# A hybrid decoder step: a later Mamba transpose, cross-attention behind the pages, longer pauses at two joins, residual loads in two parts

## The chip, the cores and the metric

The kernel runs on 1 core of a Trainium2 chip. The metric is the device time of one execution in microseconds; the time of a kernel is the median of its runs. The core has five engines with a queue of instructions each, run in order: PE (TensorE, matrix multiplication), DVE (VectorE), ACT (ScalarE), POOL (GpSimd) and SP (SyncE, which here only issues DMAs). POOL and ACT issue some DMAs too.

## The reference

One layer of a decoder step for 1024 prompt tokens and 8 sample tokens. The hidden rows are normalized and projected by `w_in`; the columns go to four head groups, each output is gated, and `w_out` and a residual follow.

```python
h = rmsnorm(x, lp['norm_g'])
p = h @ lp['w_in']
dq, dk, dvv, dg, rs, rg, mz, mxbc, mdt, xq, xg = split_in(p)
# A: differential attention (samples: over 512 paged past positions)
out_a = rmsnorm(o, subln_g) * (1 - lam_init) * silu(dg)
# B: RWKV-7, a scan over time of an 8-head state
y, rw_state_new = rwkv7_scan(rh, exp(logw), kh, vh, -kk, kk * ah, rw_state)
# M: Mamba-2, causal conv on x/B/C, then a chunked scan
ym, ssm_new = ssd_scan(xh * dt, A * dt, bh, chh, ssm_state, chunk)
# X: cross-attention into 256 memory tokens
s = einsum('bqhd,bmhd->bhqm', qx, mem_k) * D_X ** -0.5
out_x = einsum('bhqm,bmhd->bqhd', softmax(s), mem_v) * silu(xg)
x = x + concatenate([out_a, out_b, out_m, out_x]) @ lp['w_out']
# then the final rmsnorm of all rows
```

D_MODEL is 2048, each group is 512 wide, and the projection has 6792 columns.

## The kernel before

**Projections as filler.** The 1032 token columns stand in three groups of 344. Each float32 operand is split in a high and a low part (`hh`, `hl` for the activations, `whi`, `wlo` for a piece of weights), so each product takes three matmuls of 344 columns (line 565). A block is 128 output columns for all groups; a piece is a quarter of it (`KP` = 4 of 16 row tiles), loaded to `raw`, split by ACT (`whi`, line 541) and DVE (`wlo`, line 542) one piece ahead. Blocks run in the order of `ORDER`: attention's, `xq`, `rs` (RWKV), `mdt`, `mxbc`, `mz`, and last the twelve gates `xg`, `dg`, `rg`. Each block is evacuated by an `Ev...` class to DRAM. The 53 blocks of the projections (and a narrow one, `mdt`) are followed by those of `w_out`.

**Lanes and the planner.** The mixers are Python generators, called lanes. `Driver.run` lays out the program: it keeps a planned time `K.now`, which each matmul raises by its estimate (344 / 2400 us for a projection matmul), and a lane that yields a number rests for so many planned us. While no lane is due, a batch of projection matmuls is laid out (8, 4 or 10, by stage). `yield None` asks again later; `K.mark` and `K.wait` tie lanes together. So a pause becomes a number of projection matmuls between two steps of a lane in PE's queue. A scheduler then orders each engine's queue by priority and by what it takes to be ready: work whose inputs it takes to be there, DMAs above all, may stand ahead of its place in the program. Loads and splits of weights have the higher priority (`K.hi`).

**Stages.** In turn: memory and hidden rows; attention (`mixer_a`); `lane_x` (prompt's cross-attention, `mixer_x`) with `lane_sa` (`samples_a`, then `samples_x`); RWKV (`Rwkv.lanes` with `lane_b`); `lane_dt`; `lane_m` (`mixer_m`, prompt's Mamba) with `lane_s` (`samples_m`); `output`. Each stage ends when its lanes end; projections left over run on into the next, and the last of them are drained in `output`.

**What the change touches.**
- `samples_m` (from line 1375): loads `xs` (`smx`, line 1380), copies it to `v` (`smv`, lines 1381 and 1382, DVE), rests, and transposes it on PE (`p_sm`); its rows go to DRAM (`svM`) and from there the sample's state steps are fed. `mixer_m` beside it scans `r8` on DVE (line 1282), multiplies by the masked `gm` (1290, 1293), forms `xdt` (1303), and after a rest runs `p_yd` on PE from both.
- `Rwkv.products`: for each of 16 units, after the gram products, `at`, `x0`, `lt` (line 953) and `gs` are formed, then a rest, then the first join (16 matmuls to `p_t`). Four more joins follow in a loop, each after `lt` (line 973, DVE) and `rt` (line 979, ACT) and a rest.
- `samples_a`: gathers 32 pages of keys by POOL (`sakp`), multiplies and reduces each on DVE (lines 1634, 1635), six pages behind; 38 rests of 1.5 or 2.1. Then `p_sas` and the softmax. `samples_x` does the same with 16 pieces of memory keys (`sxkp`, lines 1765, 1766) and rows `sxqb` that pass through DRAM. `mixer_x` runs 16 steps: `p_xs`, softmax (`xm`, `xe`), `p_xt`, `xpt`, `p_xo`.
- PSUM: `K.ps(name, 0)` takes a buffer of a ring of three, `K.ps(name, 1)` of a ring of two.
- `output`: `residual` loads the residual rows of the first two groups (`xo`, line 1864), `evm` are the gated, mixed activations loaded and split anew (line 1873), `EvOut.rows` transposes an output block (`p_out`) and adds it to `xo`. The tiles of `xo` lie in a pool that takes the memory of the Mamba stage's pools; those of `evm` take the slots of the third group's activations, which the last block of the projections frees.

Of the kernel before, what the change touches and what calls it, by code (L numbers as in the profile page):

```python
# [11 lines left out]
F32 = mybir.dt.float32  # L12
# [819 lines left out]
class Rwkv:  # L832
# [69 lines left out]
    def products(self):  # L902
# [10 lines left out]
        for it in range(self.UNITS):  # L913
# [48 lines left out]
            for h in range(2):  # L962
                nc.vector.tensor_tensor(gs[:, h], pg[h], gm, op=ALU.mult)
            yield 4.0
            pt = ps("p_t")
# [3 lines left out]
            for l in range(4):  # L969
                xc = P.tile([128, nb, 32], F32, name="xc", tag="tm")  # L970
                nc.vector.transpose(flat(xc), pt[:, nb * 32:nb * 64])  # L971
                lt = P.tile([128, nb, 64], F32, name="lt", tag="lt")
                nc.vector.tensor_tensor(lt.rearrange("p j (k t) -> p j k t", k=2),  # L973
                                        xc.unsqueeze(2).to_broadcast([128, nb, 2, 32]),
                                        mt[:, l].rearrange("p (k t) -> p k t", k=2).unsqueeze(1).to_broadcast([128, nb, 2, 32]),
                                        op=ALU.mult)
                rt = P.tile([128, 2, nb, 32], F32, name="rt", tag="rt")
                m = 2 if l < 3 else 1
                nc.scalar.copy(rt[:, :m].rearrange("p a j t -> p (a j t)"), pt[:, :m * nb * 32])  # L979
                yield 1.6 if l else 2.2  # L980
                for b, h, q, w, n in bh:
                    K.mm(ptv[q, :m, b, :], lhsT=lt[q, b, :], rhs=rt[q, :m, b, :], start=False, stop=b == nb - 1,
                         skip_group_check=True)
# [391 lines left out]
def samples_m(K, P, dt):  # L1375
# [6 lines left out]
    nc.vector.tensor_copy(out=v[:, 32:64].rearrange("p (b s) -> p b s", b=4), in_=xs[:, 4:8, :])  # L1382
    yield 1.50
    p = K.ps("p_sm", 1)
# [201 lines left out]
def samples_a(K, P):  # L1586
# [36 lines left out]
    for i in range(32 + 6):  # L1623
# [13 lines left out]
        yield 2.1 if i >= 6 else 1.5  # L1637
    yield 2
    p = K.ps("p_sas", 0)
    for g in range(4):  # L1640
# [98 lines left out]
def samples_x(K, P):  # L1739
# [5 lines left out]
    yield 4.50  # L1745
    p = K.ps("p_sxx", 1)
    K.tp(p[:32, :128], x.rearrange("p s h -> p (s h)"), K.id)
# [20 lines left out]
    yield 8.92  # L1768
    p = K.ps("p_sxs", 1)
    for a in range(2):  # L1770
# [8 lines left out]
    yield 2.5  # L1779
    p = K.ps("p_sxw", 1)  # L1780
    for a in range(2):
# [5 lines left out]
    for b in range(8 + 3):  # L1787
# [9 lines left out]
        if b % 4 == 0:  # L1797
            po = K.ps("p_sxo", 1)
        for a in range(2):
# [4 lines left out]
        if b % 4 == 3:  # L1804
            yield from value_columns(K, P, po, o, b // 4, 1, tag="vce")
    nc.sync.dma_start(out=K.so[12:16, :, T:TT].rearrange("b p t -> p b t"), in_=o.rearrange("p (b s) -> p b s", b=4))
# [3 lines left out]
class EvOut:  # L1810


    def __init__(self, cb, xo, ss, done, fg=None, late=0.0):
        self.cb, self.xo, self.ss, self.done, self.fg, self.late = cb, xo, ss, done, fg, late

    def __call__(self, K, g, p):
# [4 lines left out]
    def rows(self, K, g, e):  # L1821
        nc, cb = K.nc, self.cb
        yield 2.0 + self.late
        q = K.ps("p_out", g % 2)
        for k in range(3):
# [20 lines left out]
def output(K, D):  # L1846
    nc, I = K.nc, K.I
    PC = 256
    with K.tc.tile_pool(name="op", bufs=1) as P:
# [6 lines left out]

        def residual():
            for g in range(2):
                for k in range(3):
                    src, n = rows[g, k]  # L1860
                    xo[g, k] = P.tile([128, 2048], F32, name=f"xo_{g}_{k}", tag="xo", bufs=6)
                    for c in range(0, 2048, 1024):
                        for p0, r, ap in src:
                            nc.sync.dma_start(out=xo[g, k][p0:p0 + r, c:c + 1024], in_=ap[:, c:c + 1024])
                        yield 4.00

        D.run([residual()], all_acc=True)
        with K.hi():
# [6 lines left out]
        def last_group():  # L1875
            yield 0.72
            for kt in kts:
                e = K.ev.tile([128, G + 3], F32, name="evm", tag="ev")[:, :G]
                nc.sync.dma_start(out=e, in_=K.sm[kt][:, 2 * G:])
                K.split_act(kt, 2, e, None)  # L1880
                yield 4.0

        def tokens(g, k, cb):
# [34 lines left out]
        def blocks():  # L1918
            K.ahead, K.more = AHEAD, P
            for cb in range(16):  # L1920
                fc = P.tile([128, 128], F32, name="fgc", tag="fgc", bufs=2)
                nc.sync.dma_start(out=fc, in_=I["final_g"][:, cb * 128:cb * 128 + 128].to_broadcast([128, 128]))
                yield from K.block(I["w_out"], cb * 128, [0, 1], EvOut(cb, tokens, ss, done, lambda cb, t=fc: t), KO_OUT)

# [15 lines left out]
            for cb in range(16):  # L1940
                if cb == FINCB:
                    while not fin:
                        yield False
                    K.large, K.ahead = (lambda: P.tile([128, 16, 128], F32, name="oraw", tag="xo", bufs=6)), 8
                yield from K.block(I["w_out"], cb * 128, [2], EvOut(cb, tokens, ss, done, gain, 4.0 if cb < 2 else 0.0),
                                   KO_OUT)
                K.turn += 1

        D.acc = blocks()
        D.run([last_group()], all_acc=True)  # L1950
        for k in range(3):
# [57 lines left out]
def lane_x(K):  # L2009

    pool = lambda n: K.tc.tile_pool(name=n, bufs=1)
    yield from K.wait("xq3", 9.00)
    with pool("xap") as P:
        a, b = mixer_x(K, P, (0, 1)), mixer_x(K, P, (2, 3))
# [124 lines left out]
```

## Time and profile before

| | |
|---|---|
| median of 3 runs | 2157.95 us (2156.27 to 2159.46) |
| the profiled execution | 2159.76 us |
| its span, first to last instruction | 2158.0 us |
| PE busy | 2088.2 us (97%) |
| DVE busy | 1145.3 us (53%) |
| ACT busy | 840.9 us (39%) |
| POOL busy | 201.7 us (9%) |
| mean granted clock of PE | 0.990 |

How to read it: "busy" is the time in which an engine had at least one instruction under way. A matmul's pipelined end is modelled, so a busy PE isn't PE at its peak. An idle time is put down to what ended last by the profile ("<-"); "issue" there means that the profile shows no releaser. The granted clock is 1.00 at PE's higher level (2.4 GHz) and 0.50 at its lower one (1.2 GHz). Of 70 us in which PE was idle, some 17 lie in the first 100 us and at the end, which the change doesn't touch.

### The profile page before, as it was taken

The numbers are of one execution on the slowest core, as the hardware profiler recorded it, in microseconds if no ns is written. First come the engines' busy times: TensorE is split into PE (matmuls) and PEld (weight loads), VectorE is DVE, ScalarE is ACT, GpSimd is POOL, SyncE is SP. The second block draws the span as 40 slices with busy tenths as digits, with TensorE's granted clock in tenths as the row PEclk, the third lists the DMA queues.
The fourth block names the chain that finished last, engine by engine and source line by source line (L and its number), as shares of the span: only waits on it lengthen the run. The fifth ranks groups of instructions, "written<-read, shape, count | busy, mean of one in ns | idle before, by whom it ended". The sixth has DMA issues, their size and how long they took to land. (4 is left out here: it accounts for less than half of the span.)

```text
span 2158.0 us, 41612 instructions
## 1 busy us (share of the span) xinstructions
PE 2088.2 (97%) x16260; PEld 1981.2 (92%) x16260; DVE 1145.3 (53%) x2795; ACT 840.9 (39%) x2231; POOL 201.7 (9%) x286
## 2 busy tenths in 40 slices
PE   8999999999999999999999999998999999999997
PEld 6799999999989999988888888897999999999997
DVE  6814353543743252258977776655865354333554
ACT  6724353443223312145455444431121144333544
POOL 2100000000721220011110001001100000000000
PEclk9999999999999999999999999998999999999998
DMA  7643435242843572333222222226544583222781
GB/s 257 194 135 87 129 88 140 78 118 68 257 144 106 154 220 68 89 85 80 74 58 67 55 62 56 58 77 159 157 136 139 153 263 106 74 69 73 241 249 53
DMA packets 336925, 263.12 MB, mean 122 GB/s; under 512 B 62204, under 2 KB 310986, under 8 KB 336032
## 3 DMA queue, kind: packets, MB, share of 16 engines
q1 hardware_dynamic: 323744, 218.64, 35.8%
q0 software_dynamic: 12320, 40.28, 6.1%
q8 instruction: 128, 2.10, 0.4%
q10 hardware_dynamic: 664, 1.54, 0.2%
q14 instruction: 69, 0.57, 0.1%
HBM read 205.65 MB, written 54.80 MB: 121 GB/s over the span
## 5 line engine op out<-in xcount | busy, mean ns | idle before, releaser
L565 PE MATMUL acc<-hh,whi 128*128 128x344 f32 x3312 | 1076.0, 325 | 8.9 <-ACT whi L541 3.0
L565 PE MATMUL acc<-hh,wlo 128*128 128x344 f32 x3312 | 1076.8, 325 | 1.6 <-DVE wlo L542 1.3
L565 PE MATMUL acc<-hl,whi 128*128 128x344 f32 x3312 | 1077.5, 325 | 0.0
L565 PEld LDWEIGHTS acc<-hh,whi 128*128 128x128 f32 x3312 | 625.2, 189 | 17.7 <-ACT whi L541 4.0
L565 PEld LDWEIGHTS acc<-hl,whi 128*128 128x128 f32 x3312 | 626.6, 189 | 4.6 <-issue 0.4
L565 PEld LDWEIGHTS acc<-hh,wlo 128*128 128x128 f32 x3312 | 624.0, 188 | 6.7 <-DVE wlo L542 3.2
L542 DVE TENSOR_TENSOR wlo<-raw,whi 128x512 fp32r<-128x512 f32 x300 | 206.9, 690 | 449.4 <-ACT whi L541 442.0
L541 ACT CAST whi<-raw 128x512 fp32r<-128x512 f32 x300 | 185.5, 618 | 473.8 <-PE acc L565 398.5
L186 PEld LDWEIGHTS p_t<-rt,lt 64*64 64x64 f32 x1280 | 44.8, 135 | 32.4 <-issue 13.7
L1831 ACT ACTIVATE p_out<-xo 128x128 f32<-128x128 f32 (+1 forms) x144 | 39.8, 277 | 78.9 <-DVE xo L1830 74.5
L186 PE MATMUL p_t<-rt,lt 64*64 64x64 f32 (+1 forms) x1280 | 54.5, 224 | 14.7 <-DVE lt L973 6.1
L1510 DVE CUSTOM_DVE_ANT_0 ae<-p_s,al 128x512 f32<-128x512 f32 (+3 forms) x96 | 49.6, 554 | 34.8 <-PE p_s L1507 34.8
L1830 DVE TENSOR_TENSOR xo<-xo,p_out 128x128 f32<-128x128 f32 (+1 forms) x144 | 39.5, 280 | 26.7 <-PE p_out L190 26.6
L1517 ACT ACTIVATE ae<-ae,am 128x128 f32<-128x128 f32 (+7 forms) x64 | 49.2, 772 | 10.9 <-DVE am L1514 10.8
L542 DVE TENSOR_TENSOR wlo<-oraw,whi 128x512 fp32r<-128x512 f32 x48 | 33.2, 692 | 31.7 <-ACT whi L541 31.4
L216 POOL TENSOR_TENSOR osr<-osr,mhalf 128x1 f32<-128x1 f32 (+1 forms) x9 | 6.0, 690 | 461.9 <-DMA xo<-in_x_prompt 337.8
L979 ACT COPY rt<-p_t 128x256 f32<-128x256 f32 x64 | 22.0, 344 | 69.5 <-DVE xc L971 66.2
L216 POOL TENSOR_TENSOR ass<-ass,mhalf 128x8 f32<-128x8 f32 x4 | 6.6, 1642 | 423.5 <-DVE ass L1558 423.5
L1618 POOL DMA_INDIRECT sakp<-in_cache_diff_k,sapt x32 | 42.4, 1326 | 31.0 <-DMA xmk<-smk 17.9
L1507 PE MATMUL p_s<-akm,aqt 128*128 128x512 f32 (+3 forms) x192 | 45.1, 359 | 0.0
L541 ACT CAST whi<-oraw 128x512 fp32r<-128x512 f32 x48 | 29.7, 618 | 32.5 <-PE acc L565 31.1
L1833 DVE TENSOR_TENSOR xo<-xo,fgc 128x128 f32<-128x128 f32 (+1 forms) x96 | 27.0, 288 | 28.6 <-ACT p_out L1831 27.6
(467 smaller groups left out, 2584.4 us busy)
## 6 DMA issues: line engine op xcount, KB each, us to landing
raw<-in_w_in SPq DMA_DIRECT2D x220, 256.0 KB
raw<-in_w_out SPq DMA_DIRECT2D x80, 256.0 KB
oraw<-in_w_out SPq DMA_DIRECT2D x12, 1024.0 KB
evm<-sm SPq DMA_DIRECT2D x48, 172.0 KB
sB<-evs SPq DMA_DIRECT2D x39, 172.0 KB
sA<-evp SPq DMA_DIRECT2D x36, 172.0 KB
evo<-so SPq DMA_DIRECT2D x36, 172.0 KB
sm<-evo SPq DMA_DIRECT2D x36, 172.0 KB
```

The lines of the kernel that those rows point to most:

```text
L186: self.nc.tensor.matmul(out, lhsT=lhsT, rhs=rhs, start=start, stop=stop, **k)
L541: nc.scalar.copy(hi, raw)
L542: nc.vector.tensor_tensor(lo, raw, hi.bitcast(F32), op=ALU.subtract)
L565: nc.tensor.matmul(acc[g][:, :G], lhsT=x[:, k, :], rhs=y, start=kp == ko[0] and k == 0 and x is hi and y is a, stop=kp == ko[-1] and k == ...
L979: nc.scalar.copy(rt[:, :m].rearrange("p a j t -> p (a j t)"), pt[:, :m * nb * 32])
L1507: nc.tensor.matmul(p[:, :k1 - k0], lhsT=qt[:, a, c], rhs=km[:, c, k0:k1], start=a == 0, stop=a == 1)
L1510: nc.vector.tensor_tensor_reduce(e[:, c, k0:k1], p[:, :k1 - k0], al[:, x0:x0 + k1 - k0], 1.0, -3e38, ALU.add, ALU.max, m[:, c, pc:pc + 1])
L1517: nc.scalar.activation(e[:, c, :nk], e[:, c, :nk], AF.Exp, bias=m[:, c, 0:1], accum_out=z[:, c:c + 1])
L1618: nc.gpsimd.indirect_dma_start(out=dst, out_offset=None, in_=I[src].rearrange("a p c -> (a p) c"), in_offset=bass.IndirectOffsetOnAxis(ap= ...
L1830: nc.vector.tensor_tensor(xt, xt, q[:n, k * 128:k * 128 + 128], op=ALU.add)
L1831: nc.scalar.activation(q[:n, k * 128:k * 128 + 128], xt, AF.Square, accum_out=self.ss[:n, 3 * g + k, cb:cb + 1])
L1833: nc.vector.tensor_tensor(xt, xt, self.fg(cb)[:n], op=ALU.mult)
```

## The change

Four edits in one:
1. `samples_m` rests 14.0 instead of 1.50 planned us ahead of `p_sm`.
2. In `Rwkv.products` the rest ahead of the first join is 5.2 instead of 4.0, that ahead of the second 2.8 instead of 2.2.
3. `samples_a` marks `sak` when its page loop is through, and `lane_x` waits for that mark. The PSUM buffers of `samples_x` move from ring 1 to ring 0.
4. `residual` takes a group as argument. Group 0 is loaded while the projections are drained, group 1 in a lane beside `last_group`; the rest after each load is 3.00 instead of 4.00. `EvOut.rows` waits until all three tiles of its group are there (`ready`).

```diff
@@ -961,7 +961,7 @@
                 nc.vector.tensor_tensor(gs[:, h], pg[h], gm, op=ALU.mult)
-            yield 4.0
+            yield 5.2
             pt = ps("p_t")
@@ -977,7 +977,7 @@
                 nc.scalar.copy(rt[:, :m].rearrange("p a j t -> p (a j t)"), pt[:, :m * nb * 32])
-                yield 1.6 if l else 2.2
+                yield 1.6 if l else 2.8
                 for b, h, q, w, n in bh:
@@ -1380,7 +1380,7 @@
     nc.vector.tensor_copy(out=v[:, 32:64].rearrange("p (b s) -> p b s", b=4), in_=xs[:, 4:8, :])
-    yield 1.50
+    yield 14.0
     p = K.ps("p_sm", 1)
@@ -1636,6 +1636,7 @@
     yield 2
+    K.mark("sak")
     p = K.ps("p_sas", 0)
@@ -1743,7 +1744,7 @@
     yield 4.50
-    p = K.ps("p_sxx", 1)
+    p = K.ps("p_sxx", 0)
     K.tp(p[:32, :128], x.rearrange("p s h -> p (s h)"), K.id)
@@ -1766,7 +1767,7 @@
     yield 8.92
-    p = K.ps("p_sxs", 1)
+    p = K.ps("p_sxs", 0)
     for a in range(2):
@@ -1777,7 +1778,7 @@
     yield 2.5
-    p = K.ps("p_sxw", 1)
+    p = K.ps("p_sxw", 0)
     for a in range(2):
@@ -1795,14 +1796,14 @@
         if b % 4 == 0:
-            po = K.ps("p_sxo", 1)
+            po = K.ps("p_sxo", 0)
         for a in range(2):
...
         if b % 4 == 3:
-            yield from value_columns(K, P, po, o, b // 4, 1, tag="vce")
+            yield from value_columns(K, P, po, o, b // 4, 0, tag="vce")
     nc.sync.dma_start(out=K.so[12:16, :, T:TT].rearrange("b p t -> p b t"), in_=o.rearrange("p (b s) -> p b s", b=4))
@@ -1810,8 +1811,9 @@
-    def __init__(self, cb, xo, ss, done, fg=None, late=0.0):
+    def __init__(self, cb, xo, ss, done, ready, fg=None, late=0.0):
         self.cb, self.xo, self.ss, self.done, self.fg, self.late = cb, xo, ss, done, fg, late
+        self.ready = ready
@@ -1821,6 +1823,8 @@
         yield 2.0 + self.late
+        while not self.ready(g):
+            yield None
         q = K.ps("p_out", g % 2)
@@ -1854,17 +1858,16 @@
-        def residual():
-            for g in range(2):
-                for k in range(3):
-                    src, n = rows[g, k]
-                    xo[g, k] = P.tile([128, 2048], F32, name=f"xo_{g}_{k}", tag="xo", bufs=6)
-                    for c in range(0, 2048, 1024):
-                        for p0, r, ap in src:
-                            nc.sync.dma_start(out=xo[g, k][p0:p0 + r, c:c + 1024], in_=ap[:, c:c + 1024])
-                        yield 4.00
-
-        D.run([residual()], all_acc=True)
+        def residual(g):
+            for k in range(3):
+                src, n = rows[g, k]
+                xo[g, k] = P.tile([128, 2048], F32, name=f"xo_{g}_{k}", tag="xo", bufs=6)
+                for c in range(0, 2048, 1024):
+                    for p0, r, ap in src:
+                        nc.sync.dma_start(out=xo[g, k][p0:p0 + r, c:c + 1024], in_=ap[:, c:c + 1024])
+                    yield 3.00
+
+        D.run([residual(0)], all_acc=True)
         with K.hi():
@@ -1879,6 +1882,8 @@
                 yield 4.0
+
+        ready = lambda g: (g, 2) in xo
@@ -1920,7 +1925,7 @@
                 nc.sync.dma_start(out=fc, in_=I["final_g"][:, cb * 128:cb * 128 + 128].to_broadcast([128, 128]))
-                yield from K.block(I["w_out"], cb * 128, [0, 1], EvOut(cb, tokens, ss, done, lambda cb, t=fc: t), KO_OUT)
+                yield from K.block(I["w_out"], cb * 128, [0, 1], EvOut(cb, tokens, ss, done, ready, lambda cb, t=fc: t), KO_OUT)
@@ -1942,12 +1947,12 @@
                     K.large, K.ahead = (lambda: P.tile([128, 16, 128], F32, name="oraw", tag="xo", bufs=6)), 8
-                yield from K.block(I["w_out"], cb * 128, [2], EvOut(cb, tokens, ss, done, gain, 4.0 if cb < 2 else 0.0),
+                yield from K.block(I["w_out"], cb * 128, [2], EvOut(cb, tokens, ss, done, ready, gain, 4.0 if cb < 2 else 0.0),
                                    KO_OUT)
...
         D.acc = blocks()
-        D.run([last_group()], all_acc=True)
+        D.run([residual(1), last_group()], all_acc=True)
         for k in range(3):
@@ -2010,6 +2015,7 @@
     yield from K.wait("xq3", 9.00)
+    yield from K.wait("sak")
     with pool("xap") as P:
```

## Rows read from the trace of the kernel before

**Rows 1.** The page, part 1: busy us (share of the span) and instructions of each engine.
```profile
PE 2088.2 (97%) x16260; PEld 1981.2 (92%) x16260; DVE 1145.3 (53%) x2795; ACT 840.9 (39%) x2231; POOL 201.7 (9%) x286
```

**Rows 2.** Stretches: length, busy of PE, PEld, DVE, ACT, POOL, granted clock, DMA share, GB/s.
```profile
550.00:600.00 50.00, 47.08 (x288) 45.30 (x287) 45.43 (x85) 12.07 (x31) 37.89 (x29) 1.00 0.88 266
600.00:650.00 50.00, 45.11 (x269) 43.68 (x268) 19.34 (x44) 15.04 (x42) 6.70 (x7) 0.97 0.40 122
750.00:800.00 50.00, 46.86 (x312) 45.59 (x311) 28.77 (x65) 9.19 (x22) 11.35 (x21) 0.97 0.68 209
...
1000.00:1050.00 50.00, 48.16 (x547) 43.02 (x541) 44.99 (x113) 25.36 (x76) 7.91 (x14) 0.97 0.29 73
...
1450.00:1500.00 50.00, 40.01 (x246) 38.76 (x245) 19.95 (x48) 7.94 (x19) 7.14 (x11) 0.86 0.57 139
```

**Rows 3.** What PE waited for, whole span: us in total, times, longest us.
```profile
PE p_sm L190 <- issue: 10.0, 1, 10.0
PE p_t L186 <- DVE lt L973: 6.1, 9, 1.8
PE p_t L186 <- DVE lt L953: 5.1, 8, 1.4
PE p_xo L186 <- ACT xpt L1728: 3.9, 1, 3.9
...
PE p_xt L190 <- issue: 2.3, 2, 1.3
...
PE acc L565 <- ACT haB L683: 2.2, 1, 2.2
PE acc L565 <- DVE evg L752: 2.2, 2, 1.6
...
PE p_t L186 <- ACT rt L979: 2.0, 2, 1.0
...
PE acc L565 <- ACT xe L1717: 0.8, 1, 0.8
```

**Rows 4.** Timeline of PE around p_sm: start us, us, engine, line, operation, [idle before].
```profile
1487.08 0.39 PE L190 MATMUL p_sm<-cst,smv 128*64 128x128 f32 x1 [9.96 <-issue]
1487.13 0.63 PE L565 MATMUL acc<-hh,whi 128*128 128x344 f32 x1
...
1493.20 0.32 PE L565 MATMUL acc<-hh,wlo 128*128 128x344 f32 x1
...
1494.30 0.32 PE L565 MATMUL acc<-hh,whi 128*128 128x344 f32 x1
1494.46 1.89 PE L186 MATMUL p_yd<-xdt,r 128*128 128x64 f32 x16
```

**Rows 5.** A stretch of 2 us behind p_sm, columns as in rows 2.
```profile
1490.00:1492.00 2.00, 2.00 (x8) 2.00 (x8) 0.51 (x1) 0.00 (x0) 0.00 (x0) 0.50 0.54 148
```

**Rows 6.** Timeline of DVE in the same place.
```profile
1486.39 0.20 DVE L1381 COPY smv<-smx 128x32 f32<-128x32 f32 x1 [7.93 <-DMA smx<-sM]
...
1488.63 0.68 DVE L1303 TENSOR_TENSOR xdt<-p_x,dt 128x512 f32<-128x512 f32 x1
```

**Rows 7.** Timeline of POOL and of SP's queue: the state loads and the load of smx.
```profile
1470.66 4.15 POOL L1417 DMA_DIRECT2D sms<-in_state_ssm  x8 [11.46 <-DVE sme L1391]
...
1471.59 0.37 SPq L1380 DMA_DIRECT2D smx<-sM  x1
```

**Rows 8.** Page loop's end, sample's memory keys (timelines); prompt's cross-attention (tile p_xs: min/median/max ns, span).
```profile
669.34 0.60 PE L190 MATMUL p_sas<-cst,sasc 128*64 128x128 f32 x4
...
778.87 1.29 DVE L1765 TENSOR_TENSOR sxkp<-sxkp,sxqb 128x512 f32<-128x512 f32 x2 [5.10 <-DMA sxqb<-svX]
...
L186 PE MATMUL p_xs<-xmk,xq x64: 377/379/484, 568.1 to 732.8; 128*128 128x256 f32 x64
```

**Rows 9.** Residual loads and loads of the mixed activations: issue ns, first and last us.
```profile
L1864 SPq DMA_DIRECT2D xo<-in_x_prompt x12: 333/458/948, 1705.8 to 1729.5; - x12
...
L1873 SPq DMA_DIRECT2D evm<-sm x32: 319/382/1376, 1742.8 to 1769.2; - x32
```

## The prediction

> **What bounds the kernel now.** I read the busy times first: TensorE (PE) is busy nearly the whole span [rows 1], and the projections' matmuls fill it wherever a side lane leaves room. Work is only moved here, none is removed, so the time can change only by what PE loses: idle stretches, and stretches at the lower of its two clocks (1.2 instead of 2.4 GHz). The table of stretches then shows where that loss lies. Of five stretches of 50 us four lose 2 to 5 us by idling and one loses 10, and four show a granted clock below 1.00 [rows 2]. The list of what PE waited for names the causes [rows 3]: one wait of 10.0 us at p_sm; 5.1, 6.1 and 2.0 us at the RWKV joins (p_t); 3.9, 2.3 (p_xo, p_xt) and 0.8 us (xe) in the cross-attention, and 2.2 us each at two evacuations (haB, evg). These groups are what the four edits can touch.
>
> I sum against the profiled execution, 2159.76 us (span 2158.0 and 1.76 outside it). It lies 1.81 us above the median 2157.95 of the runs shown; the forecast is made for the median by taking the same difference off.
>
> **Part 1: Mamba samples' transpose later.** PE stood 9.96 us in front of p_sm, from 1477.1 to 1487.1, and then ran at a granted clock of 0.50, the lower level [rows 4, 5]. Its 28 projection matmuls from 1487.13 to p_yd at 1494.46 took 7.33 us. At full clock they step by (1494.30 - 1493.20) / 7 = 0.157 us, 28 of them 4.4 us, so the half clock cost another 2.9 us. Together 12.9 us are lost here.
> The pause of 14.0 in place of 1.50 puts the transpose some 12.5 / 0.143 = 87 matmuls further back (the planner counts 344 / 2400 = 0.143 us for one), 13.7 us of PE time, behind 1490. Its own wait is then gone. But its input copies (smv) stay where they are in VectorE's queue, ahead of the pause. VectorE stood at them for 7.93 us, until 1486.39 [rows 6], for the load smx, issued at 1471.59, one us after eight state loads began to be issued [rows 7]. It lands 14.8 us after its issue. Queued on VectorE behind these copies are gm, one wlo, r and xdt, and the next PE work that needs them is p_yd: it needs xdt, 1488.63 + 0.68 = 1489.31 [rows 6]. Without p_sm's wait PE reaches p_yd after the same 28 matmuls and two small transposes, at 1477.1 + 4.4 + 0.3 = 1481.8 (or it stops a little sooner at the wlo of the next piece), and stands there 7.5 us. That wait is about as long as the old one, so I also leave the 2.9 us of half clock in. Gain: p_yd at 1489.3 instead of 1494.5, 5.2 us, less 2.9 of half clock now behind it = 2.3 us. Bounds: 0 (the new wait is as long as the old) and 12.9 (the copies hold nobody). The other instructions of the step move too: smr's store and what follows it on SP's queue, and the sample's VectorE work, go 13.7 us later, beside a later chunk of the prompt's scan; the sample has four state steps where the prompt has eight chunks, so it still ends first, and I cost it at nothing.
> By the Trainium skill, "DMA: Bandwidth & Descriptors", section "Latency and other measured facts", a DMA's fixed cost is about 2 us. By that, as an estimate, smx would be there by 1473.6, no queue would be held and the part would give back 12.9 us; the row of 14.8 us differs, and the measurement decides.
>
> **Part 2: longer pauses at two joins.** Each of 16 units waits 1.2 and 0.6 planner-us longer, 1.3 and 0.66 us of PE time (0.157 / 0.143). Line 953 belongs to the first join alone: 5.1 us, the longest wait 1.4 [rows 3]; 1.3 us more covers nearly all, -5. Lines 973 and 979 stand in a loop of four joins of which only the first gets 0.66 more: of their 8.1 us (longest 1.8) I take 3, as a wait above 0.66 is only shortened and the other three joins keep theirs. With 0.5 for the waits at p_t that name other engines: 8.5 us. Bounds: 2 (VectorE simply comes later by as much) and 13. The pauses are filled with 16 x 1.8 / 0.143 = 201 projection matmuls, 31.6 us of PE time, which were to be done later. They are not lost, but they are gone from the end: see part 4.
>
> **Part 3: cross-attention once the pages are through.** Beside the pages (VectorE 45.4 of 50 us busy [rows 2]) the cross-attention cost 3.9 + 2.3 + 0.8 = 7.0 us of waits [rows 3], and the granted clock of 0.97 over the next 50 us another 1.5. The mark comes with the end of the page loop, at the latest where p_sas stood, 669.3 [rows 8]; its 38 pauses, each rounded up to two batches of eight matmuls, fill only 38 x 16 x 0.157 = 95 us when no other lane is due between them, so it can be some tens of us earlier. The cross-attention then lasts as long as before, 568 to 733 [rows 8], so until some 805 to 835. It now runs beside the sample's memory keys, whose VectorE work began at 778.87 after a hold of 5.10 us for sxqb [rows 8]. That stretch already lost 3.1 us and 1.5 of clock on its own [rows 2]. This is the new collision: 16 pieces where the first had 32, so half of 8.5, 4.25, and a little for the hold: 5. Net gain 8.5 - 5 = 3.5 us. Bounds: 8.5 (no new wait) and -4 (the hold of 5.1 us falls on the cross-attention's joins as well). The other PSUM ring keeps the two lanes from waiting for each other's buffers; three buffers serve where at most two are held, at no cost. The later cross-attention delays nobody: the sample's memory values still follow, and the gates that read its output are the last twelve blocks of the projections.
>
> **Part 4: residual loads in two parts.** Before, twelve loads were issued from 1705.8 to 1729.5, and the 32 loads of the mixed activations (evm) from 1742.8 to 1769.2 [rows 9]. With half of them later, the waits at evg in this stretch (2.2 us [rows 3]) should go. But part 2 has taken 31.6 us of projections from between the scans' end and the last block. The residual loads can't start before the scans' memory is free, so relative to evm they start at 1705.8 + 31.6 = 1737.4. If six go ahead of evm they take half of 23.7 us, 11.9, of which 1742.8 - 1737.4 = 5.4 lie before evm: evm is late by 6.4 us. If evm passes them, by 0. I take 3, the middle, since both queue on SP and neither row shows who goes first: net cost 3 - 2.2 = 1 us. Bounds: a gain of 2.2 us and a cost of 18.3 (all twelve ahead, 23.7 - 5.4) with 2.9 of half clock after it. The wait for `ready` holds only the second group's transposes of the first column block, some us; PE has the next block meanwhile.
> The Trainium skill, same page, section "Queues, rings and completion order", has each DMA engine consume one issuing queue's descriptors in ring order; that speaks against this part, as loads issued ahead of evm on SP's queue can't be passed; no row above separates it.
>
> **Sum.** 2.3 + 8.5 + 3.5 - 1 = 13.3 us: 2159.76 - 13.3 = 2146.5 for the profiled execution, 2144.7 for the median. Predicted 2145.
>
> **Rivals.**
> (a) VectorE is not held, or its queue has the copies behind xdt: part 1 gives 12.9. For it: the pauses shift every lane. Against: the copies' place depends on the load, which is not moved. 2144.7 - 10.6 = 2134. The fixed cost that the Trainium skill states, under part 1, would lead here.
> (b) The join waits are VectorE's lateness and follow the longer pauses: part 2 gives 2 instead of 8.5. For it: VectorE is busy 45.0 of 50 us in the stretch from 1000 [rows 2], and a longer pause also lets other lanes' work in. Against: the longest wait is 1.8 us, near the pause added [rows 3]. 2151.
> (c) The cross-attention collides with the memory keys as hard as it can: part 3 gives -4. Against: the collision lasts half as long. 2144.7 + 7.5 = 2152.
> (d) Slower: all residual loads stand in SP's queue ahead of evm, and PE waits at the first output block. It costs 18.3 + 2.9 instead of 1, so 2144.7 + 20.2 = 2165, and decides from a delay of some 14 us of evm on, where the other gains are used up. For it: the loads are issued as soon as their memory is free, the spare projections are gone. Against: only six come first in the program. The ring order that the Trainium skill states, under part 4, would lead here.
> That the change doesn't do what it says is in (a) to (c): a pause that moves a wait and not its cause.
>
> **How the numbers follow.** Forecast 0.53, (a) 0.15, (b) 0.12, (c) 0.12, (d) 0.08. A measurement of this kernel can tell some 0.2% (4.3 us) from no change. The forecast, (a) and half of what (b) and (c) spread over are faster by more: 0.53 + 0.15 + 0.12 = 0.80; the other half, with part 4's cost on top, 0.12 within; (d) 0.08 slower. The range takes in (a) below, at 2132 with the other parts a little better, and (b) and (c) together with some us of part 4 above, 2158; (d) and the ends of several bounds at once are left out.
>
> **What would show it.** Part 1: p_sm without a wait, and in the same place a wait of 5 to 8 us at p_yd or wlo that VectorE's smv copies end; none would prove (a). Part 2: the waits at line 953 gone, those at 973 and 979 reduced by a third or more; the first gate block within the RWKV stage. Part 3: no waits at p_xo and p_xt near 550 to 610, some beside sxkp. Part 4: the residual and evm loads adjoining, a wait of some us at the first output block. A wait above 14 us there, or unchanged waits at the joins, would make the prediction wrong.

## The result and the profile after

The changed kernel takes 2168.66 us (median of 5 runs, 2167.04 to 2169.57); the kernel before took 2157.09 us beside it. The ratio is 1.0061, with a 95% interval of 1.0048 to 1.0074: 13 us slower, where 13 us faster was forecast. The profiled execution took 2167.04 us, with a span of 2165.2 us.

What PE waited for, whole span of the kernel after (us in total, times, longest us), against [rows 3]:
```profile
PE p_bt L190 <- DVE gm L1290: 9.0, 2, 7.9
PE acc L565 <- ACT hh L383: 8.5, 1, 8.5
PE p_t L186 <- DVE lt L973: 4.3, 4, 1.9
PE p_xt L190 <- DVE xe L1721: 3.8, 2, 3.6
```
The wait at p_sm is gone, and one of 7.9 us at p_bt stands in its place. The group of line 953 is gone, and of the 13.2 us at the joins 4.3 are left in the list. A wait of 8.5 us at hh, which the kernel before did not have, is new.

Three stretches of [rows 2], and those where the new waits lie (length, busy of PE, PEld, DVE, ACT, POOL, granted clock, DMA share, GB/s):
```profile
550.00:600.00 50.00, 44.03 (x274) 42.88 (x273) 42.97 (x75) 6.76 (x14) 36.88 (x28) 1.00 0.82 251
...
750.00:800.00 50.00, 46.16 (x276) 44.72 (x275) 31.73 (x63) 13.52 (x37) 9.37 (x18) 0.97 0.74 230
...
1450.00:1500.00 50.00, 50.00 (x480) 46.98 (x479) 21.06 (x52) 14.70 (x41) 5.01 (x5) 1.00 0.33 89
1500.00:1550.00 50.00, 40.95 (x260) 39.85 (x259) 24.74 (x52) 9.65 (x21) 4.71 (x9) 0.93 0.55 140
...
1750.00:1800.00 50.00, 36.97 (x201) 34.56 (x200) 19.28 (x44) 16.77 (x44) 0.00 (x0) 0.83 0.82 250
```
The last line is the result: between 1750 and 1800, where the projections end and the output blocks begin, PE is idle for 13 us and has a granted clock of 0.83. In the same stretch the kernel before was busy for 49.44 us at a clock of 1.00:
```profile
1750.00:1800.00 50.00, 49.44 (x318) 49.08 (x317) 31.39 (x75) 28.68 (x74) 0.00 (x0) 1.00 0.63 196
```

The stages shift against each other in time, so I also compared them by work: PE's work is counted in the mean step, from start to start, that each kind of matmul has in the trace of before, and what PE takes beyond that over the same amount of work is its loss. Worked out so from the traces, in us, for four stages of the same work in each kernel (the zero is arbitrary, only differences down a column count):

| kernel | parts | pages, cross-attention | RWKV | Mamba | to the output blocks |
|---|---|---|---|---|---|
| before | none | 16.0 | 41.7 | 15.0 | -4.1 |
| part 1 alone | 1 | 11.3 | 43.9 | 13.0 | -3.9 |
| part 3 alone | 3 | 13.9 | 45.0 | 11.2 | -5.2 |
| pauses undone | 1, 3, 4 | 21.1 | 42.3 | 5.0 | -3.6 |
| pauses alone | 2 | 9.9 | 36.4 | 15.8 | 20.0 |
| after | 1 to 4 | 14.1 | 35.8 | 13.4 | 13.9 |

The last row less the first is the account of the change: -1.8, -5.9, -1.6 and **+18.0 us at the change to the output blocks**, with another -1.6 in the memory stage at the start, which the change doesn't touch; together 7.1 from unrounded values, the difference of the two spans (2165.2 - 2158.0 = 7.2).

How PE came to wait there is read from three queues of the kernel after. First PE (start us, us, engine, line, operation, [idle before]):
```profile
1776.83 0.66 PE L565 MATMUL acc<-hh,whi 128*128 128x344 f32 x1 [8.53 <-ACT hh L383]
...
1779.09 0.66 PE L565 MATMUL acc<-hh,whi 128*128 128x344 f32 x1 [0.77 <-ACT evy L1820]
```
Then ScalarE, which makes this hh, and VectorE, which makes the last gate block's rows (evo):
```profile
1758.68 0.98 DVE L753 SCALAR_TENSOR_TENSOR evo<-evg,evo 128x344 f32<-128x344 f32 x2 [1.15 <-DMA evo<-so]
...
1776.30 0.48 ACT L383 CAST hh<-evm 128x344 fp32r<-128x344 f32 x1 [10.80 <-DMA evm<-sm]
```
And SP's queue between the two:
```profile
1758.34 0.50 SPq L1867 DMA_DIRECT2D xo<-in_x_prompt  x1
1760.57 0.38 SPq L525 DMA_DIRECT2D raw<-in_w_out  x1
1760.99 0.50 SPq L1867 DMA_DIRECT2D xo<-in_x_prompt  x1
1763.15 0.38 SPq L525 DMA_DIRECT2D raw<-in_w_out  x1
1763.57 0.51 SPq L1867 DMA_DIRECT2D xo<-in_x_prompt  x1
1766.25 0.38 SPq L525 DMA_DIRECT2D raw<-in_w_out  x1
1766.67 0.50 SPq L1867 DMA_DIRECT2D xo<-in_x_prompt  x1
1767.22 1.01 SPq L754 DMA_DIRECT2D sm<-evo  x1
1768.27 0.38 SPq L1867 DMA_DIRECT2D xo<-in_x_prompt  x1
1768.70 0.39 SPq L754 DMA_DIRECT2D sm<-evo  x1
1773.87 0.33 SPq L1876 DMA_DIRECT2D evm<-sm  x1
```
The evo rows are made by 1759.7; their two stores go out 7.5 and 9.0 us later. Between lie three weight pieces, each of which waits for a buffer until VectorE has split an earlier piece (5.4 us in all on SP's queue; that split follows ScalarE's, which waits for PE), and the residual loads that follow them. The last evm load reads what the first of the two stores wrote (the second holds the third group's rows). It is issued as soon as that store has landed, 6.7 us after the store's issue, and lands at 1776.3. PE waits for it, and then runs at the lower clock for a while, granted 0.56 and 0.58 in these stretches:
```profile
1770.00:1780.00 10.00, 2.40 (x6) 1.70 (x7) 1.21 (x2) 1.44 (x3) 0.00 (x0) 0.56 0.69 197
1780.00:1790.00 10.00, 8.70 (x38) 8.15 (x37) 1.23 (x3) 1.30 (x3) 0.00 (x0) 0.58 0.97 295
```
The residual loads are issued from 1758.3 on; before, they ran from 1705.8 to 1729.5 [rows 9].

### The profile page after: what moved, and what is told of

Read it like the earlier page. It is cut to its first block, busy times and chain, and to the rows that moved or that the text cites. A ratio compares the mean times of both kernels' runs of the same rounds, so it can differ in the third digit from the quotient of the medians.

```text
span 2165.2 us, 41599 instructions
## 1 busy us (share of the span) xinstructions
PE 2091.7 (97%) x16260; PEld 1981.5 (92%) x16260; DVE 1145.9 (53%) x2795; ACT 840.5 (39%) x2231; POOL 203.7 (9%) x286
## 5 line engine op out<-in xcount | busy, mean ns | idle before, releaser
L186 PEld LDWEIGHTS p_t<-rt,lt 64*64 64x64 f32 x1280 | 43.9, 134 | 22.4 <-issue 13.2
L542 DVE TENSOR_TENSOR wlo<-oraw,whi 128x512 fp32r<-128x512 f32 x48 | 33.2, 692 | 31.6 <-ACT whi L541 31.4
```

The source lines that it names most:

```text
L186: self.nc.tensor.matmul(out, lhsT=lhsT, rhs=rhs, start=start, stop=stop, **k)
L542: nc.vector.tensor_tensor(lo, raw, hi.bitcast(F32), op=ALU.subtract)
```

## The experiments

Ratios are against the kernel before on the same chip, with 95% intervals; 1.0061 is the mark of the changed kernel.

### Which part: the pauses undone, the pauses alone, part 4 undone

Pauses undone (parts 1, 3, 4):
```
-            yield 5.2
+            yield 4.0
-                yield 1.6 if l else 2.8
+                yield 1.6 if l else 2.2
```


> The changed kernel with part 2 undone (pauses 4.0 and 2.2 as before), parts 1, 3 and 4 kept. Theory Q: the order on SP's queue round the last gate block is that of the kernel before, so no wait of 8 us at the first output block; parts 1 and 3 give their 3.3 + 1.7 us: 2150 to 2154. The waits at the joins (line 953) return, some 5 us, in the same place as before. Theory S (part 4 alone is to blame): 2160 to 2168, with the wait for hh still there.

Measured: 0.9977 (0.9964 to 0.9990), 2156.7 us, some 3 us above what the theory of the queue (Q) had. The wait at hh is gone; the list of what PE waits for between 1735 and 1830 has one entry:
```profile
PE acc L565 <- DVE evg L752: 2.6, 2, 1.8
```
The pauses alone, put into the kernel before:

> The kernel before with part 2 alone (pauses 5.2 and 2.8). Theory Q: the wait for hh of about 8 us at the first output block and the half clock round it are there without parts 1, 3 and 4, some 16 to 18 us, against some 6 us gained at the joins: 2165 to 2172. Theory S: no such wait, the joins' gain of some 6 us stays: 2150 to 2152. Theory T: some us of wait, 2155 to 2165.

Measured: 1.0083 (1.0064 to 1.0103). The loss is there without the other parts (8.3 us at hh, and 7.4 us at whi behind it). At 2178.5 us it is larger than the theory of the queue had it, 2165 to 2172:
```profile
PE acc L565 <- ACT hh L383: 8.3, 1, 8.3
PE acc L565 <- ACT whi L541: 8.2, 2, 7.4
```
The changed kernel with part 4 undone (`residual` and `ready` are as in the kernel before):
```
-        D.run([residual(0)], all_acc=True)
+        D.run([residual()], all_acc=True)
...
-        D.run([residual(1), last_group()], all_acc=True)
+        D.run([last_group()], all_acc=True)
```


> The changed kernel with part 4 undone: all twelve residual loads issued ahead of the evm loads, as before; parts 1 to 3 kept. Theory Q (the loss at the change to the output projection comes from part 2: the longer pauses push the opening of the output stage behind the last gate block, so that on SP's queue the stores of that block's gated rows, sm<-evo, stand behind weight pieces that wait for a buffer; part 4 is nearly idle): the queue's order around the stores stays as it is, so 2165 to 2172, and PE still waits some 8 us for hh at the first output block. Theory T (transfers: residual loads and evm loads share the DMA engines, and evm lands late by the residual bytes ahead of it): twelve loads ahead in place of six, some 6 us and more slower than the changed kernel, 2174 or more. Theory S (part 4 itself, its split or its wait for the second half, costs the time): back to about 2150.

Measured: 1.0087 (1.0065 to 1.0109). At 2178.3 us it isn't back at 2150, as it would be if part 4 were the cause (S); it lies where the theory of the transfers (T) had it, above the 2165 to 2172 of the theory of the queue. The loss by work at the output blocks is 19.3 us instead of 13.9, with a second wait of 7.3 us at whi. So part 4 is not the cause. It rather took some 5 us off a loss that part 2 makes, though the interval touches that of the changed kernel; my value for "part 4" was the price of part 2.

### The shift alone, and its size

The kernel before with one longer pause, away from the joins:
```
-    yield 7.50
+    yield 47.50
     p = K.ps("p_sst", 1)
```


> The kernel before with one pause lengthened, ahead of the last state's transpose (p_sst) of the prompt's scan, from 7.5 to 47.5: some 44 us of projection matmuls more are drawn ahead of the scans' end, and no join is touched. If the loss comes from the scans' end (and so the memory of the output stage) moving toward the end of the projections, it is here as in the kernel with the pauses alone, some 20 us, without the joins' gain of 6: 2175 to 2182. If it came from the joins or the stage round them, nothing: 2157 to 2161.

Measured: 1.0101 (1.0080 to 1.0122), 2179.12 us, 21 us above the kernel before beside it. No join is touched, nothing is added, and the loss is there, in the same place:
```profile
PE acc L565 <- ACT hh L383: 8.9, 1, 8.9
PE acc L565 <- ACT whi L541: 4.4, 1, 4.4
```
This is the cause proper: the projection matmuls that pauses draw forward are missing at the end. How many are missing can be counted in the order of PE's instructions, as the projection matmuls that stand behind the scans' last transposes (p_cv): 408 in the kernel before, 120 after. The shift is 288 matmuls, 45 us, not the 201 of the forecast. Each pause ends at a whole batch of four: 4.0 / 0.143 gives 28 matmuls, 5.2 / 0.143 gives 36.4, so 40; 2.2 gives 16 and 2.8 gives 20. That makes 16 per unit, 256 in all. Of the other 32, 4 are missing with part 3 alone too (404 left); the rest I did not trace.

Half the shift, by a pause of 27.5:

> The kernel before with the pause ahead of p_sst at 27.5 (7.5 before; 47.5 cost 20 us): 272 projection matmuls (43 us of PE time) are left between the scans' end and the output blocks, against 408 in the kernel before (no loss), 192 and 120 or 132 in those that lost 16 to 21 us. If the loss begins only once the residual rows (24 us from their first to their last issue in the kernel before) and evm (26 us) no longer fit one after the other ahead of the output blocks, some 50 us, a part of it is here: 2163 to 2170. If it needs less room: 2157 to 2160.

Measured: 1.0058 (1.0044 to 1.0072), 2172.2 us, above the 2163 to 2170 expected, with 10.7 us more loss than before at the output blocks. With 272 matmuls left PE waits a stage earlier, at the accumulator of the last gate block, and ScalarE shows why: its reading of that accumulator (line 751) stands behind conversions, the first of which waits for a load.
```profile
1763.92 2.81 ACT L383 CAST hh<-evm 128x344 fp32r<-128x344 f32 x6 [3.70 <-DMA evm<-sm]
1766.63 1.14 ACT L751 ACTIVATE evg<-acc 128x344 f32<-128x344 f32 x3
...
1767.76 0.66 PE L565 MATMUL acc<-hh,whi 128*128 128x344 f32 x1 [10.12 <-DVE evg L752]
```
The first of the two pauses alone (5.2), in the kernel before:

> The kernel before with the pause ahead of the first join alone (5.2 in place of 4.0; the second stays at 2.2). The waits at line 953 go, some 5 us. If the shift decides by its size, in proportion: half to three quarters of the 21 us lost with both pauses remain, 2162 to 2170. If there is a reserve (the stretch from 1705 to 1763 between the scans' end and the last block) and the loss begins only past it: 2152 to 2157.

Measured: 1.0058 (1.0040 to 1.0076); 192 matmuls are left. The group of line 953 is gone, but the stage as a whole gains nothing (43.6 us by work, before 41.7): PE waits elsewhere in it.
```profile
PE p_yt L190 <- DVE y L1088: 3.8, 3, 1.8
PE p_yt L190 <- ACT ld L773: 3.5, 2, 2.1
```
By the number of matmuls left (408, 272, 192, 132, 124) the loss over the kernel before is 0, 10.7, 19.4, 21.4 and, with the pauses alone, 24.1 us. There was no free reserve: two thirds of 408 is already too little.

### Bytes or order

The residual loads kept in number and place, at 64 of 1024 columns (this leaves most of the residual out of the result):
```
-                        nc.sync.dma_start(out=xo[g, k][p0:p0 + r, c:c + 1024], in_=ap[:, c:c + 1024])
+                        nc.sync.dma_start(out=xo[g, k][p0:p0 + r, c:c + 64], in_=ap[:, c:c + 64])
+                    nc.gpsimd.memset(xo[g, k][:, c + 64:c + 1024], 0.0)
```


> The changed kernel with the residual loads kept in number and place, but of 64 columns each in place of 1024 (the remaining columns are set to zero on GpSimd, so most of the residual is left out of the result): 5.2 MB less to move, the same order on SP's queue. Theory T: the loss at the change to the output projection goes, 2149 to 2154. Theory Q: the order is what costs, the wait of 8 us for hh stays, 2164 to 2170.

Measured: 1.0004 (0.9990 to 1.0019), 0.6% below the changed kernel; at 2157.6 us it is far from the 2164 to 2170 that the order alone would have kept. The order on SP's queue is the same, and the stores still go out 4 to 5 us after evo is made (1762.1), but the round trip behind the first of them, which the load reads, is short:
```profile
1766.17 0.51 SPq L754 DMA_DIRECT2D sm<-evo  x1
...
1769.13 0.37 SPq L1877 DMA_DIRECT2D evm<-sm  x1
...
1772.08 0.43 PE L565 MATMUL acc<-hh,whi 128*128 128x344 f32 x1 [1.61 <-ACT hh L383]
```

With the residual bytes in, 6.7 us lie between that store and the load that reads it (1767.22 to 1773.87); with the bytes out, 3.0 us. From 1735 to 1810 the DMA engines move 17.47 MB in the changed kernel (mean 233 GB/s), 14.66 MB in the kernel before, which had issued its residual loads by 1730. So bytes are a part of it. The Trainium skill, "DMA: Bandwidth & Descriptors", section "Latency and other measured facts", has a fixed cost of some 2 us for a DMA; the 3.0 us lie 1 us above it, and the residual bytes go with another 3.7 us here. The ring order of its section "Queues, rings and completion order", which stood behind rival (d), agrees with this pair; the pair does not tell it from transfers that share the bandwidth, and that loads "can't be passed" was my own step from it.

The gate blocks' stores on another queue:
```
-        nc.sync.dma_start(out=K.sm[j][:, a:a + G], in_=o)
+        nc.gpsimd.dma_start(out=K.sm[j][:, a:a + G], in_=o)
```


> The changed kernel with the gate blocks' stores sm<-evo issued from GpSimd's queue instead of SP's. Theory Q: the last block's two stores go out at about 1760, as soon as VectorE has made them (1758.7 and 1759.6 in the trace of after), in place of 1767.2 and 1768.7; the last evm lands at about 1768; PE's wait of 8.5 us and most of the 17 us of half clock round it go: 2150 to 2156. Theory T: the stores are small, evm still waits for the residual bytes: 2165 to 2170. Theory S: unchanged, 2165 to 2170.

Measured: 1.0069 (1.0048 to 1.0090), 2178.0 us: my theory of the stores' order alone (2150 to 2156) falls, and the other two, with 2165 to 2170, did not have this time either. The wait at hh shrinks to 0.5 us, and one of 12.8 us at whi comes behind it. ScalarE makes whi, and stands at a conversion of the third group, whose load is late and which nobody needs for another 200 us:
```profile
1799.21 0.48 ACT L383 CAST hh<-evm 128x344 fp32r<-128x344 f32 x1 [16.04 <-DMA evm<-sm]
...
1804.13 0.65 PE L565 MATMUL acc<-hh,whi 128*128 128x344 f32 x1 [12.77 <-ACT whi L541]
```
Both parts of the residual loads behind evm:
```
-        D.run([residual(0)], all_acc=True)
+        D.run([], all_acc=True)
...
-        D.run([residual(1), last_group()], all_acc=True)
+        D.run([residual(0), residual(1), last_group()], all_acc=True)
```


> The changed kernel with both parts of the residual loads issued behind the evm loads (none ahead of them). Theory T (from 1735 to 1810 the DMA engines are the limit: 17.5 MB are moved in 75 us in the trace of after, 5.5 MB of them residual rows, which the longer pauses have pushed into the same stretch as evm and the first output weights): evm and the weights, which PE waits for, come first, and most of the 16 to 18 us go: 2150 to 2157. Theory Q (order: the last gate block's stores stand on SP's queue behind weight pieces that wait for a buffer): the stores still stand behind two such pieces, 2160 to 2168.

Measured: 1.0054 (1.0035 to 1.0074), no better than the changed kernel, where the theory of the transfers had 2150 to 2157. The wait at hh is down to 0.5 us here too, and again a wait on ScalarE takes its place: the copy evy, which frees PE's accumulator, follows a conversion of the third group.
```profile
1773.13 0.42 PE L565 MATMUL acc<-hh,whi 128*128 128x344 f32 x1 [0.48 <-ACT hh L383]
...
1781.55 0.66 PE L565 MATMUL acc<-hh,whi 128*128 128x344 f32 x1 [7.29 <-ACT evy L1820]
...
1780.67 0.48 ACT L383 CAST hh<-evm 128x344 fp32r<-128x344 f32 x1 [5.91 <-DMA evm<-sm]
1781.06 0.79 ACT L1820 COPY evy<-acc 128x344 f32<-128x344 f32 x2
```
So I moved the third group as well; first both moves together, then the third group alone:
```
         def last_group():
-            yield 0.72
+            yield 40.0
```


> The changed kernel with both parts of the residual loads behind evm, and the third group's evm loads and their conversions on ScalarE begun 40 planner-us later (in place of 0.72). In the kernel with the residual loads moved alone, PE's wait at hh went from 8.5 us to 0.5, and a wait of 7.3 us at evy came in its place: ScalarE's queue held the copy that frees PE's accumulator behind a conversion whose load (third group, not needed for another 240 us) had not landed. If the residual bytes ahead of it are all that is left, this wait and the half clock after it go: 2152 to 2158. If the transfers themselves are still the limit (evm and the first weights late whatever the order), PE waits somewhere else for about as long: 2163 to 2168.

Measured: 0.9992 (0.9982 to 1.0002), 2157.25 us, 0.7% below the changed kernel. From 1750 to 1800 82% of the DMA engines' time is taken, as before the edit, and no byte is left out; only what PE needs first goes first. The stores go out as soon as evo is made (1761.8), and the longest wait left is 2.1 us, at a granted clock of 1.00.
```profile
1761.87 0.81 SPq L754 DMA_DIRECT2D sm<-evo  x2
...
1765.27 0.33 SPq L1876 DMA_DIRECT2D evm<-sm  x1
...
1791.07 0.43 PE L565 MATMUL acc<-hh,whi 128*128 128x344 f32 x1 [2.11 <-ACT evy L1820]
...
1750.00:1800.00 50.00, 45.26 (x286) 44.06 (x285) 24.38 (x59) 21.33 (x60) 0.00 (x0) 1.00 0.82 254
```


> The changed kernel with the third group's evm loads and conversions 40 planner-us later, and the residual loads left where the change puts them. The last gate block's stores stay on SP's queue behind the weight pieces and the residual loads between them. If that order makes the wait of 8.5 us for hh, it stays, and only some 3 us that follow it go: 2163 to 2168. If the third group's transfers were what made evm late, the wait goes: 2153 to 2160.

Measured: 1.0021 (1.0006 to 1.0036). The wait at hh stays, 7.6 us, as for the order on SP's queue; what followed it goes. Each move alone brings less (0.1%, which can't be told from nothing, and 0.4%), both together 0.7%: behind the first late load stands a second.
```profile
1781.15 0.66 PE L565 MATMUL acc<-hh,whi 128*128 128x344 f32 x1 [7.57 <-ACT hh L383]
```

### Parts 1 and 3

Part 1 alone:

> The kernel before with part 1 alone (p_sm's pause 14.0 in place of 1.50). If VectorE's copies happen to stand behind what PE needs next, as in the kernel without the pauses, the wait of 10 us and its half clock go: some 10 us of PE time in this stage, 2146 to 2151. If VectorE is held ahead of gm and xdt as in the changed kernel, 2 us: 2154 to 2158.

Measured: 0.9984 (0.9973 to 0.9995), a gain of 3.5 us (1.1 to 5.8). PE's wait has moved to p_bt, 7.9 us, as in the changed kernel. In that one, VectorE shows what it waits for:
```profile
1524.56 0.20 DVE L1381 COPY smv<-smx 128x32 f32<-128x32 f32 x1 [8.84 <-DMA smx<-sM]
...
1524.74 0.42 DVE L1290 TENSOR_TENSOR gm<-p_g,cst 128x256 f32<-128x256 f32 x1
...
1525.21 0.69 PE L190 MATMUL p_bt<-cst,mxb 128*128 128x128 f32 x2 [7.95 <-DVE gm L1290]
```
Without the pauses the order on VectorE is another (gm ahead of the copies), and there the stage loses only 5.0 us by work instead of 15.0. That was seen in the one kernel with parts 1, 3 and 4, and is luck of the order, not a property of part 1: the kernel with part 1 alone has the hold again.

The copies on GpSimd, in the changed kernel:
```
-    nc.vector.tensor_copy(out=v[:, 0:32]..., in_=xs[:, 0:4, :])
-    nc.vector.tensor_copy(out=v[:, 32:64]..., in_=xs[:, 4:8, :])
+    nc.gpsimd.tensor_copy(out=v[:, 0:32]..., in_=xs[:, 0:4, :])
+    nc.gpsimd.tensor_copy(out=v[:, 32:64]..., in_=xs[:, 4:8, :])
```


> The changed kernel with the two copies smv, which wait for the load smx, on GpSimd in place of VectorE. If they are what held gm, and by it PE at p_bt for 7.95 us with 6.8 us of half clock, both go: some 8 to 10 us less, 2158 to 2161. If gm waits for something else (its own loads, the scan), no change: 2166 to 2170.

Measured: 1.0038 (1.0025 to 1.0051), 0.23% or 5 us below the mark, about half of the 8 to 10 expected. GpSimd takes the wait, gm runs early, and the wait at p_bt falls to 0.6 us. One of 2.6 us for a gate load (mxg) and one of 1.5 us at p_my take a part of it back. By work the stage loses 9.6 us instead of 13.4.
```profile
1515.35 0.40 DVE L1290 TENSOR_TENSOR gm<-p_g,cst 128x256 f32<-128x256 f32 x1
...
1519.51 0.24 POOL L1381 COPY smv<-smx 128x32 f32<-128x32 f32 x1 [9.05 <-DMA smx<-sM]
```
Part 3 alone:

> The kernel before with part 3 alone (cross-attention once the pages are through, the samples' PSUM buffers from the other ring). By the forecast, a gain of 3.5 us: 2153 to 2156. By the loss of PE time in this stage in the kernels run so far (12.8 us on average without part 3, 17.0 with it), a cost of some 4 us: 2160 to 2164, with a wait of 3.6 us at p_xt beside the memory keys.

Measured: 0.9996 (0.9985 to 1.0006): no difference that can be told, against both numbers expected. The waits of [rows 3] at p_xo and xe are gone and the collision is there, at p_xt:
```profile
PE p_xt L190 <- DVE xe L1721: 5.2, 2, 3.6
```
By work this stage loses 9.9 to 18.8 us in seven kernels without part 3 and 11.2 to 21.1 in eleven with it (means 13.9 and 15.5). One execution's loss varies here by more than the part could give, and my expectation of a cost of 4 us was read from too few of them.

### Together

Both moves and the copies on GpSimd, in the changed kernel, and the same without part 3:

> The changed kernel with three edits together: residual loads behind evm, the third group's evm 40 planner-us later, and the smv copies on GpSimd. The first two took 15 us off the changed kernel, the third alone 5. If the two losses are apart in time and independent: 2150 to 2154, ahead of the kernel before. If the reserve of the last stage swallows what is won earlier: 2156 to 2160.

> The same as the kernel with the three edits together, but without part 3 (cross-attention beside the pages, as before). Part 3 alone gave no difference that could be told from none (ratio 0.9996, 0.9985 to 1.0006). If it is idle, within 3 us of that kernel; by the loss of PE time in its stage (some 3 us more with it on average), 2147 to 2151 and faster than it.

Measured: 1.0004 (0.9990 to 1.0018) with part 3, 0.9980 (0.9969 to 0.9991) without. The gain of the copies did not add to that of the moves, and I did not find where it went. The time is the one expected if the last stage swallows it, but the loss at the output blocks is the same with and without the copies moved (within 0.2 us by work); by work the Mamba stage is better by 2.4 us, and the RWKV stage, which neither edit touches, is worse by 1.8 in that execution. The second of these is ahead of the kernel before by 0.2%, some 4 us, and so are the kernels with the pauses undone (0.9977) and with part 1 alone (0.9984). No version beats the kernel before by more than 0.23%. The two kernels of this section are 3 us apart, at the edge of what I had set for an idle part 3, and their intervals touch: whether part 3 costs something here stays open.

## Why the prediction was wrong

**Part 1: right, but for the place.** The wait left p_sm and came back as one of 7.9 us that VectorE's copies end; 7.5 was forecast. It stands at p_bt instead of p_yd or wlo: p_bt waits for gm, which is queued behind the copies, and comes ahead of p_yd. Gain: 1.6 us by work in the changed kernel, 2.0 alone (3.5 by the times); 2.3 was forecast. Rival (a), 12.9 us, needs the copies behind gm; the order with the pauses undone came near it (10.0 by work), and moving them to GpSimd gave 5 us.

**Part 2: the joins right in kind, a little small; its other half missed.** Line 953 is gone as forecast, 973 and 979 went from 8.1 to 4.3 us in the lists. Over eleven kernels with both pauses and six without any, the RWKV stage loses 36.8 and 43.3 us: a gain of 6.5, forecast 8.5. Rival (b), 2 us, falls. The 5 us that I gave to line 953 are not shown, though: with the first pause alone the stage gained nothing in its one execution. But the sentence "they are not lost, but they are gone from the end" held the larger number. The size of the shift was off (45 us for 31.6; whole batches of four make 40 of it), and its price was taken as 3 us.

**Part 3: wrong in size.** Forecast 3.5, measured nothing: 0.9996. The collision beside the memory keys came as forecast (3.6 us at p_xt, with 5 taken for it). The gain did not: the 8.5 us that I read for the old place came from one execution, and other kernels without part 3 lose up to 6 us less in the same stage.

**Part 4: the step that failed.** I took evm to be late by 3, "the middle" between 0 and 6.4, and cost the part at 1 us net. The runs showed a loss of 18.0 us at the change to the output blocks in its place, and that it belongs to what part 2 takes from the end: the shift alone makes it (1.0101), the pauses undone take it away, part 4 undone does not. Two things were wrong in the working. I looked at when evm would be *issued* and not at what else is queued there: 31 of the 32 evm loads in PE's way were in fact issued ahead of the residual rows, which began at 1758.3 where I had 1737.4, and the last one, with the store that it reads, held PE. And I compared only residual loads with evm, where the weight pieces, the third group and the stores share the same queue: the stretch had been filled already, with a DMA share of 0.89 in the kernel before, so 45 us less of room could hardly be free:
```profile
1710.00:1770.00 60.00, 57.82 (x365) 57.15 (x364) 28.70 (x58) 23.13 (x51) 0.00 (x0) 1.00 0.89 278
```
The sign that I had set there, one wait above 14 us, did not come: the longest is 8.5 us, and shorter waits and the lower clock are the rest.

**Rival (d)** named the place, the sign and nearly the time (2165 us; measured 2168.7), and got 0.08. That the time came so near is in part luck: the loss was 18.0 us and not 18.3 + 2.9, and the other parts gave less than forecast. Its mechanism was half right: not all residual loads stand ahead of evm; five are enough, ahead of its last load, four of them ahead of the store which that load reads. Against it I had written that "only six come first in the program"; the kernel with none ahead of evm was no faster, since the same lateness then came through ScalarE's queue. The bound of 18.3 was in the sum from the start. I took the middle between 0 and 6.4 instead, though, as I wrote, no row showed "who goes first".

## What to carry to other kernels

A pause that is filled with work from elsewhere isn't free: count the instructions that it draws forward, in whole batches, and look at what they covered where they came from, above all loads. Where an in-order queue (a DMA queue, or an engine that converts what is loaded) holds work that is needed now and work that is needed much later, put the later work later; moving one of two such blocks shows little as long as the second still stands there (0.1 and 0.4% here, both 0.7%). A stall read from one execution is a sample: before its removal is counted as a gain, see whether other traces of the same code have it.

## What the runs showed of the hardware

The last evm load on SP's queue, which reads what a store on the same queue just wrote, was issued 3.0 us after the store with the residual bytes out, 3.0 us with the residual loads behind evm and 3.4 us with both moves. With residual rows ahead of the store it was 6.7 us in the changed kernel and 8.0 us with the third group alone moved. In all five traces the load went out within 0.02 us of the store's landing.

A stand of 8.5 us left PE at a lower clock for some ten us more: granted 0.56 and 0.58 from 1770 to 1790 in the changed kernel. With a stand of 7.3 us (residual loads behind evm) the same two stretches have 0.82 and 0.67. In the trace with both moves, whose longest stand there is 2.1 us, it stays at 1.00.
